# The gated delta rule of a fused kernel: from heads to tiles, from half-array to whole-array products, and part of it moved among the projections

## The chip, the cores and the metric

One core of one Trainium2 chip runs the whole program. The metric is the device time of one execution in microseconds (us), as the median of three runs. TensorE (PE) multiplies matrices, VectorE (DVE), ScalarE (ACT) and GpSimd (POOL) do the elementwise work, SyncE (SP) issues the DMAs. Each engine works through its own instructions in the order in which they were written into the program, and semaphores make it wait for others.

## What is computed

A block of two layers (gated linear attention, retention) over 2048 rows of 1024 channels, and then a second block, in which one projection feeds two branches: a gated delta rule with 4 heads of 128, in chunks of 64 rows, and an attention with 4 heads in which each row uses only the 256 keys that an index scores highest. The change is in the second block; cut to what matters:

```python
def gated_deltanet(qkv, z, b, a, conv_w, a_log, dt_bias, g_norm):
    qkv = silu(causal_conv(qkv, conv_w)); q, k, v = split(qkv, 3)
    q = l2norm(heads(q)) * DK ** -0.5; k = l2norm(heads(k)); v = heads(v)
    beta = sigmoid(b); g = -exp(a_log) * softplus(a + dt_bias)
    gc = cumsum(g, axis=-1)                 # within a chunk of 64
    decay = exp(where(causal, gc_i - gc_j, -inf))
    kb, vb = k * beta, v * beta
    lmat = where(strict, (kb @ k.T) * decay, 0)
    tmat = inverse(lmat + eye)              # triangular solve
    u, w = tmat @ vb, tmat @ (kb * exp(gc))
    attn = (q @ k.T) * decay
    qg, kg, glast = q * exp(gc), k * exp(gc_last - gc), exp(gc_last)
    def step(S, (qg, kg, u, w, attn, gl)):  # chunk after chunk
        v_new = u - w @ S
        o = qg @ S + attn @ v_new
        return S * gl + kg.T @ v_new, o
    o = rmsnorm(scan(step, 0)) * silu(z)

def dsa_sparse_attention(q_b, ckv, iq, ik, iw, ...):
    score = sum_h iw * relu(iq @ ik.T); sel = top_k(score, 256)
    p = softmax(q_b @ ckv[sel].T * R ** -0.5 + bias); o = (p @ ckv[sel]) @ w_uv * silu(z)
```

## The kernel before

The first block ends at about 1634 us of the trace. The second block (`layer2`) goes over four quarters q0 to q3 of 512 rows. In each, `begin` loads and turns the rows; `chains` makes 28 projections, each 24 matmuls of 128x512 (three per slice of 128 channels: high part by high part, low by high, high by low, so that float32r products add up to float32), and each is taken out of PSUM by ACT; then `delta` and `attention` run together; then `output` multiplies by the last weight. Weights come by DMA into buffers `wh` and `wl`, five and six of them, one projection ahead of use by the code (`ahead`), and earlier where buffers are free.

`weave` merges generators: at each turn the one that is least far along, by its steps over the number given with it, makes the next step. In `layer2` the PE's order is kept as written while projections run (`manual_schedule`); in the weave of `delta` and `attention` a scheduler places instructions. The other engines' order is the scheduler's throughout. Three weaves of projections run beside the index's scores (`index_scores`) and the search for the 256th highest score (`select`), which works on blocks 0 and 1 of a quarter, then on 2 and 3, mostly on DVE. A search ends with two `If`s for each block (L1523, L1525), which repair rare cases; DVE loads a flag and branches. What follows in DVE's order, the masks `mk` that ACT makes of the result (L1585) and with them the attention, comes behind. In the third weave (projections from number 19 or 20 to 28, 8 steps each) `start` waits until 14 steps are left, and then makes the first step of `attention` and of `delta`: loads and set-up alone, no product.

The attention goes through four blocks of 128 rows and four heads: score products L1610 into two banks `ix` (three matmuls for each piece of up to 512 keys), on DVE the sum with the mask and the maximum (L1612), on ACT the exponential; PE turns the result (L1631) and multiplies by the keys (L1641).

`delta` works head by head: for a head and all four tiles of 128 rows, `first` to `fourth` complete the inverse (L1882, L1894), turn v and k (L1890, L1907), and make u and w (L1913, L1920). When all heads are done, the recurrence runs over 4 tiles of two chunks (`cc` 0 and 1). In a chunk and for all four heads: `ws`, both w and q by the state S (L1966, 128 rows by 128 columns of the array); `vnew` on DVE, a head at a time (L1970), in the 64 partitions of this chunk; then `us`, k by vnew, on 64 rows (L1977) and `oa`, attn by vnew, on 64 rows and 64 columns (L1980), written in two loops and alternating in PE's order; then the new state on DVE (L1983). `norms` (L1263) sums squares for each head of q and k by products with one column of ones, 16 of them on 64 columns of the array each.

Of the kernel before, what the change touches and what calls it, by code (L numbers as in the profile page):

```python
# [44 lines left out]
PACE = [(6, 3, 30, 30, 14, 40)] * 4  # L45
# [16 lines left out]
class Builder:  # L62
# [784 lines left out]
    def group_b(self, ctx):  # L847
        self.pools(ctx, "b", {"pj": 2, "ix": 2, "tp": 2, "mm": 2}, 1, dict(wh=5, wl=6))
# [123 lines left out]
    def layer2(self, src, dst):  # L972
# [3 lines left out]
        self.n_g2 = 9  # L976
# [42 lines left out]
        for h in range(4):  # L1019
# [9 lines left out]
        nc.vector.memset(St, 0.0)  # L1029

        self.k = dict(cw=cw, hist=hist, nega=nega, dtb=dtb, ltri=ltri, mneg=mneg, blk=blk, chk=chk,
                      img=img, ggd=ggd, gs=gs, sh=sh, gkv=gkv, ckvN=ckvN, ckvH=ckvH, ckvL=ckvL, ikH=ikH, ikL=ikL, Tb=Tb, wuv=wuv,
                      mod=mod, src=src, dst=dst, S=St, zsel=zsel, gsel=gsel, iota=iota, under=under)
        self.mk = self.mkp.tile([P, 2048], BF16, name="mk")
        for q in range(NQ):
            pace = PACE[q]
            with self.tc.manual_schedule(engines={mybir.EngineType.PE}):
# [9 lines left out]
                self.weave((self.chains(q, st, range(x[2], 28)), 8 * (28 - x[2])), (self.select(q, st, (2, 3)), pace[3]), (self.start(att, delta, 8 * (28 - x[2]) - pace[4]), 60))  # L1047
            n = sum(4 * (1 + -(-max(0, i - 1) // 4) + 2 * -(-(i + 1) // 4)) for i in range(4 * q, 4 * q + 4))
            self.weave((delta, pace[5]), (att, n))
# [4 lines left out]
    @staticmethod  # L1054
    def image(m, h):


        return bass.AP(tensor=m.tensor, offset=m.offset + 4 * h * 129 * P, ap=[[P, P], [129 * P, 4], [1, P]])

# [20 lines left out]
    def start(self, *streams):  # L1080

        *streams, n = streams
        for _ in range(n):
            yield
        for s in streams:
            next(s)
            yield
# [89 lines left out]
    def chains(self, q, st, which):  # L1177
# [6 lines left out]
        seq += [(n, cb) for n in ("v", "za", "qb", "zb") for cb in range(4)]  # L1184
# [67 lines left out]
    def norms(self, st, h):  # L1252
# [15 lines left out]
        br, br2 = st["br"][:, :, h], st["br2"][:, :, h]  # L1268
        v.tensor_copy(st["rr"][:, :, h], r)
        v.tensor_tensor(out=br, in0=st["beta"][:, :, h], in1=r[:, 0:4], op=ALU.mult)  # L1270
        v.tensor_tensor(out=br2, in0=br, in1=r[:, 0:4], op=ALU.mult)
# [442 lines left out]
    def gates(self, st, sm):  # L1714
# [21 lines left out]
        st.update(beta=beta, g=g.rearrange("p t h -> p (t h)"), br=t16("br"), br2=t16("br2"))  # L1736

    def decays(self, st):
# [7 lines left out]
        for cc in range(2):  # L1746
            nc.tensor.matmul(gp[64 * (1 - cc):64 * (1 - cc) + 64, 64:80], c["ltri"][:, 64 * cc:64 * cc + 64], g2, start=True, stop=True)
# [4 lines left out]
        gx = self.small([P, 5, 16], "gx", bufs=1)  # L1752
        v.tensor_copy(gx, gp[:, :80].rearrange("p (j x) -> p j x", j=5))
        v.tensor_tensor(out=gx[:, 1, :], in0=gx[:, 1, :], in1=gx[:, 0, :], op=ALU.subtract)
        ge = self.small([P, 5, 16], "ge", bufs=1)
# [6 lines left out]
    def delta_products(self, st, h):  # L1762
# [17 lines left out]
        for ti in range(4):  # L1780
            sl = slice(ti * P, (ti + 1) * P)
            v.scalar_tensor_tensor(out=dc[:, sl], in0=qk[:, sl], scalar=st["rr"][:, ti, h:h + 1], in1=dc[:, sl], op0=ALU.mult, op1=ALU.mult)
# [37 lines left out]
    def delta(self, q, st):  # L1820

        nc, c = self.nc, self.k
        v = nc.vector
        sp, S = st["sp"], c["S"]
        beta, ge, n2, rr = (st[n] for n in ("br", "ge", "n2", "rr"))
        col = lambda t, ti, h: t[:, 4 * ti + h:4 * ti + h + 1]
        egc = ge[:, 0, :].rearrange("p (t h) -> p t h", h=4)
        ekg, nbeta, rin, rq = (self.small([P, 4, 4], n, bufs=1) for n in ("ekg", "nbeta", "rin", "rq"))
        for o, x, y in ((ekg, ge[:, 1, :].rearrange("p (t h) -> p t h", h=4), rr[:, 0:4, :]), (rin, n2[:, 0:4, :], rr[:, 0:4, :])):
            v.tensor_tensor(out=o, in0=x, in1=y, op=ALU.mult)  # L1830
# [94 lines left out]
        for h in range(4):  # L1925
            yield
            if h < 3:
                load(h + 1)
# [144 lines left out]
```

## Time and profile before

| what | value |
|---|---|
| median of three runs | 3402.31 us (3400.49 to 3407.59) |
| profiled execution | 3399.2 us, its span 3397.2 us |
| mean granted TensorE clock | 0.968 |
| PE busy | 3232.6 us, 95% of the span |
| DVE, ACT, POOL busy | 1921.7, 1178.5, 1065.1 us |
| q0: projections / attention and delta rule | 1633.9 to 1833.7 / to 1953.5 us |
| q1 | 2002.0 to 2231.7 / to 2370.2 us |
| q2 | 2424.0 to 2671.2 / to 2814.5 us |
| q3 | 2876.0 to 3137.4 / to 3319.6 us, the end at 3397.2 |

The table is read from the times, the page's first part, and from where the last matmul of the projections (L1190) and the first of the output (L210) start. A matmul of float32 is two records in the trace, one of float32r is one; a busy time of PE has overlap in it, so that prices are best read from the distance between starts.

### The profile page before, as it was taken

To read this page: it belongs to the slowest core of one execution; us is meant where nothing else is said; L and a number is where in the kernel's file an instruction comes from. 1 tells how busy PE (TensorE), PEld (TensorE's weight loads), DVE (VectorE), ACT (ScalarE), POOL (GpSimd) and SP (SyncE) were. 2 spreads that over 40 slices of the span, in tenths; PEclk is the share of its full clock that TensorE was granted. 3 is DMA by queue.
4 is the path that set the end of the run, shared out by engine and by line. 5 is a ranking of instruction groups with operands and counts; after the bars stand their busy time and mean duration, and the time that the engine had idled before them with its cause. 6 is when DMAs were issued, how large, how long until landed. Compare 5 with 4: busy or idle time off the path is not lost. (4 is left out here: it accounts for less than half of the span.)

```text
span 3397.2 us, 46405 instructions
## 1 busy us (share of the span) xinstructions
PE 3232.6 (95%) x16946; PEld 2625.8 (77%) x16946; DVE 1921.7 (57%) x5192; ACT 1178.5 (35%) x1977; POOL 1065.1 (31%) x917
## 2 busy tenths in 40 slices
PE   8999999999989999999998999979998999998898
PEld 5878877788877787878787778767786778776877
DVE  2236455244514742245576557865588865698953
ACT  4222243122322322212332324334254443553542
POOL 3123361232553546452221122512116112134111
PEclk9999999999999999999998899989999999999899
DMA  4112247123536725212668255652545705436302
GB/s 123 34 44 97 96 138 269 48 81 115 186 98 217 265 88 192 93 48 101 219 232 246 65 198 193 198 166 80 174 165 166 210 14 187 167 131 209 99 32 75
DMA packets 352727, 472.39 MB, mean 139 GB/s; under 512 B 80867, under 2 KB 235699, under 8 KB 351446
## 3 DMA queue, kind: packets, MB, share of 16 engines
q1 hardware_dynamic: 352470, 469.20, 42.2%
q8 instruction: 133, 2.18, 0.3%
q14 instruction: 124, 1.02, 0.1%
HBM read 365.13 MB, written 103.99 MB: 138 GB/s over the span
## 5 line engine op out<-in xcount | busy, mean ns | idle before, releaser
L144 POOL TENSOR_TENSOR wl<-wr,wh 128x1024 fp32r<-128x1024 f32 x126 | 299.8, 2383 | 561.7 <-ACT wh L143 550.2
L210 PE MATMUL pj<-wh,xh 128*128 128x512 f32 x1024 | 403.0, 396 | 10.5 <-ACT wh L143 9.6
L210 PE MATMUL pj<-wl,xh 128*128 128x512 f32 x1024 | 404.2, 395 | 3.8 <-POOL wl L144 3.8
L199 PE MATMUL pj<-xh,wh 128*128 128x512 f32 x992 | 397.9, 401 | 8.3 <-ACT wh L143 5.9
L210 PE MATMUL pj<-wh,xl 128*128 128x512 f32 x1024 | 403.1, 394 | 0.0
L199 PE MATMUL pj<-xh,wl 128*128 128x512 f32 x992 | 393.7, 397 | 0.0
L199 PE MATMUL pj<-xl,wh 128*128 128x512 f32 x992 | 393.6, 397 | 0.0
L1190 PE MATMUL pj<-xh,wh 128*128 128x512 f32 x896 | 360.3, 402 | 17.7 <-ACT spl L1217 9.4
L1190 PE MATMUL pj<-xl,wh 128*128 128x512 f32 x896 | 355.9, 397 | 9.9 <-DVE xl L165 3.8
L1190 PE MATMUL pj<-xh,wl 128*128 128x512 f32 x896 | 354.8, 396 | 0.0
L143 ACT CAST wh<-wr 128x1024 fp32r<-128x1024 f32 x126 | 130.5, 1038 | 438.9 <-PE pj L210 143.5
L210 PEld LDWEIGHTS pj<-wh,xh 128*128 128x128 f32 x1024 | 193.8, 189 | 53.3 <-ACT wh L143 10.4
L199 PEld LDWEIGHTS pj<-xh,wh 128*128 128x128 f32 x992 | 183.8, 185 | 61.5 <-ACT wh L143 7.7
L210 PEld LDWEIGHTS pj<-wl,xh 128*128 128x128 f32 x1024 | 193.9, 189 | 45.5 <-POOL wl L144 5.8
L210 PEld LDWEIGHTS pj<-wh,xl 128*128 128x128 f32 x1024 | 193.9, 189 | 40.6 <-issue 0.8
L199 PEld LDWEIGHTS pj<-xl,wh 128*128 128x128 f32 x992 | 183.7, 185 | 46.2 <-issue 4.5
L199 PEld LDWEIGHTS pj<-xh,wl 128*128 128x128 f32 x992 | 183.3, 185 | 45.8 <-issue 3.2
L1190 PEld LDWEIGHTS pj<-xh,wh 128*128 128x128 f32 x896 | 170.7, 191 | 56.0 <-ACT spl L1217 10.2
L1190 PEld LDWEIGHTS pj<-xl,wh 128*128 128x128 f32 x896 | 170.9, 191 | 47.3 <-DVE xl L165 5.6
L1353 ACT ACTIVATE relu<-ix 128x512 f32<-128x512 f32 (+3 forms) x266 | 143.3, 543 | 184.8 <-PE ix L1347 122.2
L1354 DVE SCALAR_TENSOR_TENSOR score<-relu,iwc,score 128x512 f32<-128x512 f32 (+3 forms) x266 | 191.7, 721 | 19.5 <-ACT relu L1353 16.3
L1190 PEld LDWEIGHTS pj<-xh,wl 128*128 128x128 f32 x896 | 170.7, 190 | 37.8
(542 smaller groups left out, 6479.7 us busy)
## 6 DMA issues: line engine op xcount, KB each, us to landing
wh<-kh SPq DMA_DIRECT2D x140, 512.0 KB, 4.4
wl<-kl SPq DMA_DIRECT2D x140, 512.0 KB, 5.0
wr<-in_l_w_in_dram SPq DMA_DIRECT2D x92, 512.0 KB, 3.7
kh<-wh SPq DMA_DIRECT2D x37, 512.0 KB, 3.6
kl<-wl SPq DMA_DIRECT2D x37, 512.0 KB, 4.5
wr<-in_l_w_out_dram SPq DMA_DIRECT2D x32, 512.0 KB, 3.6
x<-y SPq DMA_DIRECT2D x32, 512.0 KB, 2.6
wr<-in_w_in_dram SPq DMA_DIRECT2D x29, 512.0 KB, 4.8
```

The costliest lines, as they stand in the source:

```text
L143: nc.scalar.copy(wh, raw)
L144: nc.gpsimd.tensor_tensor(out=wl, in0=raw, in1=f(wh), op=ALU.subtract)
L199: self.nc.tensor.matmul(ps[:m, :], a[:, k, :], b[tb][k], start=(n == 0), stop=(n == 3 * KT - 1))
L210: self.nc.tensor.matmul(ps, a[tb][k][:, o:o + P], b[:, k % 2, :], start=(n == 0), stop=(n == 3 * KT - 1))
L1190: nc.tensor.matmul(ps, a[:, k, :], b[0][k], start=k + n == 0, stop=k == KT - 1 and n == 2)
L1353: nc.scalar.activation(t[:, :m], ps[:, :m], AF.Relu)
L1354: nc.vector.scalar_tensor_tensor(out=o, in0=t[:, :m], scalar=w, in1=o, op0=ALU.mult, op1=ALU.add)
```

## The change

The delta rule goes tile by tile: for a tile of 128 rows and all four heads `first` to `fourth` prepare, and the recurrence of a tile follows its own preparation, with the next tile's four preparing steps placed between its chunk's steps. `us` takes all 128 rows: k is kept in two copies, `kg0` and `kg1`, each with zeros in the rows of the other chunk, and `vnew` lies in two fixed buffers of 128 partitions. `oa` is made once for a tile, on 128 rows and 128 columns, after its second chunk. `vnew` is one subtraction for all heads on DVE, since beta now stands in the factors of k, `attn` and u; u leaves PSUM by an ACT copy. `norms` takes 8 products on 128 columns instead of 16 on 64; `decays` loses two products. The loads go by tile too. `wh` and `wl` lose one buffer each, and small buffers go from 9 to 11. In the third weave `part` waits 4 steps and then makes 10 steps of `attention`, and waits 20 and then makes 6 of `delta`; these use the banks `ix` where `delta` used `pj`. The projection of `qb` moves ahead of `za`.

```diff
-PACE = [(6, 3, 30, 30, 14, 40)] * 4
+PACE = [(6, 3, 30, 30, 10, 40, 20, 6)] * 4
...
-        self.pools(ctx, "b", {"pj": 2, "ix": 2, "tp": 2, "mm": 2}, 1, dict(wh=5, wl=6))
+        self.pools(ctx, "b", {"pj": 2, "ix": 2, "tp": 2, "mm": 2}, 1, dict(wh=4, wl=5))
...
-                self.weave((self.chains(q, st, range(x[2], 28)), 8 * (28 - x[2])), (self.select(q, st, (2, 3)), pace[3]), (self.start(att, delta, 8 * (28 - x[2]) - pace[4]), 60))
...
+                self.dtag = "ix"
+                m = 8 * (28 - x[2])
+                self.weave((self.chains(q, st, range(x[2], 28)), m), (self.select(q, st, (2, 3)), pace[3]),
+                           (self.part(att, 4, pace[4]), 4 + pace[4]), (self.part(delta, pace[6], pace[7]), pace[6] + pace[7]))
+            self.dtag = "pj"
+            self.weave((delta, 40 - pace[7]), (att, sum(n) - pace[4]))
...
-        seq += [(n, cb) for n in ("v", "za", "qb", "zb") for cb in range(4)]
+        seq += [(n, cb) for n in ("v", "qb", "za", "zb") for cb in range(4)]
...
-                for cc in range(2):
-                    o = 64 * (cc ^ n)
-                    nc.tensor.matmul(ss[o:o + 64, 4 * n + ti:4 * n + ti + 1], sq[:, ti * P + 64 * cc:ti * P + 64 * cc + 64],
-                                     self.ones[:, 0:1], start=True, stop=True)
+                nc.tensor.matmul(ss[:, 4 * n + ti:4 * n + ti + 1], sq[:, ti * P:(ti + 1) * P], self.ones[:, 0:1], start=True, stop=True)
...
+            for o, x in ((T["k"], egc), (T["kg0"], ekg[:, 0]), (T["kg1"], ekg[:, 1])):
+                v.tensor_tensor(out=h4(o), in0=h4(tp), in1=by_head(x, ti), op=ALU.mult)
...
+        for fn in (first, second, third, fourth):
+            fn(0)
+            yield
...
-                vn = self.g2("vnew")
-                for h in range(4):
-                    sl = slice(h * P, (h + 1) * P)
-                    v.scalar_tensor_tensor(out=vn[a, sl], in0=ws[a, sl], scalar=nb2[a, 4 * ti + h:4 * ti + h + 1],
-                                           in1=UB[h][a, ti * P:(ti + 1) * P], op0=ALU.mult, op1=ALU.add)
-                nc.scalar.copy(on[b, :], ws[b, :])
+                v.tensor_tensor(out=vn[a, :], in0=T["ub"][a, :], in1=ws[a, :], op=ALU.subtract)
+                nc.scalar.copy(on[a, :], ws[b, :])
                 yield
-                us = self.psum("pj")
-                for h in range(4):
-                    sl = slice(h * P, (h + 1) * P)
-                    nc.tensor.matmul(us[:, sl], KG[h][a, ti * P:(ti + 1) * P], vn[a, sl], start=True, stop=True)
-                for h in range(4):
-                    sl = slice(h * P, (h + 1) * P)
-                    nc.tensor.matmul(oa[b, sl], AT[h][a, ti * P + 64 * cc:ti * P + 64 * cc + 64], vn[a, sl], start=True, stop=True)
+                for fn in itertools.islice(ahead_of, 1):
+                    fn(ti + 1)
+                    yield
+                us = self.psum(self.dtag)
+                for sl in heads:
+                    nc.tensor.matmul(us[:, sl], T["kg0" if cc == 0 else "kg1"][:, sl], vn[:, sl], start=True, stop=True)
...
+                if cc == 1:
+                    oa = self.psum("mm")
+                    for sl in heads:
+                        nc.tensor.matmul(oa[:, sl], T["at"][:, sl], vn[:, sl], start=True, stop=True)
```

How the instructions of three places move. In the rows a name before the arrow is what is written, those behind it are read; a number at a name's end tells buffers apart, xN is N of the same, and ISA is an instruction that the listing has no name for. First PE in q0's recurrence, one chunk of four heads before (`us` L1977, `oa` L1980):

```order
L1977 MATMUL pj_14610<-vnew_14589,kg_14223 128x128
L1980 MATMUL mm_14583<-vnew_14589,at_14220 64x128
L1977 MATMUL pj_14610<-vnew_14589,kg_14223 128x128
L1980 MATMUL mm_14583<-vnew_14589,at_14220 64x128
L1977 MATMUL pj_14610<-vnew_14589,kg_14223 128x128
L1980 MATMUL mm_14583<-vnew_14589,at_14220 64x128
L1977 MATMUL pj_14610<-vnew_14589,kg_14223 128x128
L1980 MATMUL mm_14583<-vnew_14589,at_14220 64x128
L1631 MATMUL tp_15002<-ident,P_14730 128x128 x3
L1966 MATMUL pj_14629<-dS_14619,wq_14210 128x128 x2
```

and after the change (`ws` L1950, `us` L1959, `oa` L1968; L1879 to L1906 prepare the next tile, L1619 is the attention):

```order
L1950 MATMUL pj_14481<-dS_14418,dt_14295 128x128 x4
L1879 MATMUL pj_14515<-T_14471,ms_14469 128x64 x4
L1959 MATMUL pj_14526<-vnew_11744,dt_14295 128x128 x4
L1886 MATMUL pj_14542<-ident,v_14475 128x128 x4
L1890 MATMUL pj_14548<-Y_14473,T_14471 128x64 x4
L1950 MATMUL pj_14570<-dS_14531,dt_14295 128x128 x4
L1619 MATMUL ix_14560<-ckvH,qh_14501 128x128
L1619 MATMUL ix_14565<-ckvH,qh_14501 128x256
L1900 MATMUL pj_14582<-ident,k_14477 128x128 x4
L1619 MATMUL ix_14560<-ckvH,ql_14502 128x128
L1619 MATMUL ix_14560<-ckvL,qh_14501 128x128
L1619 MATMUL ix_14565<-ckvH,ql_14502 128x256
L1619 MATMUL ix_14565<-ckvL,qh_14501 128x256
L1968 MATMUL mm_14613<-vnew_11744,at_14448 128x128 x4
L1906 MATMUL pj_14591<-v_14475,Y_14473 128x128 x4
L1959 MATMUL pj_14603<-vnew_11744,kg_2041_14397 128x128 x4
```

The alternation of two products is gone; `us` stands four in a row, `oa` four in a row behind every second one, with preparation and attention in between.

Second, PE in q3 where the projections end: before, all of the attention's score products (L1610) stand behind the last projection (L1190):

```order
L1190 MATMUL pj_30152<-xh_26645,wh_30094 128x512
L1190 MATMUL pj_30152<-xl_26647,wh_30094 128x512
L1523 UNCONDITIONAL_BRANCH
L1190 MATMUL pj_30152<-xh_26645,wl_30095 128x512
L1523 UNCONDITIONAL_BRANCH
L1610 MATMUL ix_30923<-ckvH,qh_30178 128x512
L1610 MATMUL ix_30928<-ckvH,qh_30178 128x512
L1610 MATMUL ix_30923<-ckvH,ql_30179 128x512
L1610 MATMUL ix_30923<-ckvL,qh_30178 128x512
L1610 MATMUL ix_30928<-ckvH,ql_30179 128x512
```

After, the third score product of the first head (L1619, bank `ix_29785`) stands within the fourth projection from the end (L1202); some 93 matmuls of projections follow it:

```order
L1202 MATMUL pj_29781<-xl_26446,wh_29708 128x512
L1202 MATMUL pj_29781<-xh_26444,wl_29709 128x512
L1532 UNCONDITIONAL_BRANCH x2
L1619 MATMUL ix_29785<-ckvH,qh_29615 128x384
L1619 MATMUL ix_29785<-ckvH,ql_29616 128x384
L1619 MATMUL ix_29785<-ckvL,qh_29615 128x384
L1202 MATMUL pj_29781<-xh_26444,wh_29708 128x512
L1202 MATMUL pj_29781<-xl_26446,wh_29708 128x512
```

The first two score products are earlier still. The bank of the third is that of the first, `ix_29671`, and DVE must have read that. Third, DVE's order after the change at that place: the first reading of `ix_29671` (L1621) stands behind both `If`s of blocks 0 and 1 (L1532, L1534):

```order
L1534 UNCONDITIONAL_BRANCH x2
L1532 UNCONDITIONAL_BRANCH
L1529 ISA x2
L1387 TENSOR_TENSOR t_s_29399<-t_s_29399,t_sl_29400 128x2
L1621 ISA P_29669,at_mx_29670<-ix_29671,mk 128x512
L1621 ISA at_mx_29670 128x1
L1621 ISA P_29669,at_mx_29670<-ix_29746,mk 128x512
L1621 ISA at_mx_29670 128x1
```

So a product that stood behind the projections now stands among them, and still behind the same `If`s.

## Rows read from the trace of the kernel before

**Rows 1.** Four windows: bounds, length, busy us (count) by engine, PEclk, DMA share, GB/s.

```profile
1833.70:1953.50 119.80, 100.11 (x589) 81.49 (x588) 58.62 (x217) 38.86 (x116) 23.69 (x29) 0.79 0.36 111
2231.70:2370.20 138.50, 121.40 (x782) 104.22 (x781) 85.67 (x315) 55.48 (x135) 24.39 (x26) 0.88 0.31 92
2671.20:2814.50 143.30, 134.84 (x963) 117.30 (x962) 105.66 (x371) 72.16 (x151) 25.03 (x27) 0.96 0.32 98
3137.40:3319.60 182.20, 161.48 (x1139) 143.25 (x1137) 132.21 (x434) 93.92 (x175) 29.07 (x31) 0.91 0.26 78
```

**Rows 2.** Timeline of PE, q0: start, busy us, line, tiles, rows*columns, shape, count.

```profile
1925.44 1.06 PE L1966 MATMUL pj<-dS,wq 128*128 128x128 f32 x8
1926.34 0.83 PE L1641 MATMUL mm<-PT,ckvN 128*128 128x128 f32 x6
1927.10 0.48 PE L1977 MATMUL pj<-vnew,kg 64*128 64x128 f32 x2
...
1930.20 0.66 PE L1945 MATMUL pj<-ident,on 128*128 128x128 f32 x4
```

**Rows 3.** Timeline of PE, q0, an earlier chunk.

```profile
1895.41 0.79 PE L1977 MATMUL pj<-vnew,kg 64*128 64x128 f32 x2 [0.45 <-DVE vnew L1970]
...
1900.75 1.65 PE L1966 MATMUL pj<-dS,wq 128*128 128x128 f32 x6
```

**Rows 4.** Timeline of PE, q3, eight records of L1977 in a run.

```profile
3265.28 1.16 PE L1977 MATMUL pj<-vnew,kg 64*128 64x128 f32 x8
3266.37 0.43 PE L1980 MATMUL mm<-vnew,at 64*64 64x128 f32 x2
```

**Rows 5.** Timeline of PE, q0, products of decays and of norms between projections.

```profile
1672.82 0.29 PE L1745 MATMUL tp<-gg__1641_11966,ltri 128*128 128x16 f32 x2
...
1673.71 0.29 PE L1747 MATMUL tp<-gg__1641_11966,ltri 128*64 128x16 f32 x4
...
1701.37 0.39 PE L1190 MATMUL pj<-xl,wh 128*128 128x512 f32 x1
1701.59 0.39 PE L1190 MATMUL pj<-xh,wl 128*128 128x512 f32 x1
1701.91 1.10 PE L1263 MATMUL tp<-ones,ext 128*64 128x1 f32 x32
1702.94 0.50 PE L1190 MATMUL pj<-xh,wh 128*128 128x512 f32 x1
```

**Rows 6.** DVE by line, 1833.7 to 3319.6 us: busy, mean ns, idle ahead.

```profile
L1970 DVE SCALAR_TENSOR_TENSOR vnew<-pj,nbeta,ub 64x128 f32<-64x128 f32 x128 | 37.2, 348 | 22.9 <-PE pj L1966 22.6
L1983 DVE SCALAR_TENSOR_TENSOR dS<-dS,ge,pj 128x128 f32<-128x128 f32 x128 | 35.9, 344 | 60.6 <-PE pj L1977 60.6
...
L1211 DVE TENSOR_TENSOR iq<-pj,iq 64x512 fp32r<-64x512 f32 x24 | 16.5, 690 | 25.5 <-ACT iq L1210 25.3
```

**Rows 7.** ACT by line, from 1633.9 us on.

```profile
L1234 ACT ACT_TABLE_LOAD x8 | 10.3, 1283 | 0.1
```

**Rows 8.** PE's waits in q0's window: total, times, longest us.

```profile
PE ix L1610 <- DVE at_mx L1612: 11.6, 1, 11.6
```

**Rows 9.** Timeline of DVE, q0, where PE waits in rows 8.

```profile
1846.81 0.29 DVE L1612 CUSTOM_DVE_ANT_0 P<-ix,near 128x128 f32<-128x128 f32 x1 [13.04 <-DMA T<-img]
```

**Rows 10.** Timelines of PE and DVE, q2, behind the first pair's search.

```profile
2658.86 0.50 PE L1190 MATMUL pj<-xh,wh 128*128 128x512 f32 x1 [3.81 <-ACT spl L1217]
...
2661.03 0.17 DVE L1383 TENSOR_SCALAR t_m<-t_dc 128x2 int32<-128x2 f32 x1 [2.82 <-DVEq L1523]
```

**Rows 11.** Timelines of PE and DVE, q3, behind the first pair's search.

```profile
3137.40 0.39 PE L1190 MATMUL pj<-xh,wl 128*128 128x512 f32 x1
3151.83 1.22 PE L1610 MATMUL ix<-ckvH,qh 128*128 128x512 f32 x2 [14.04 <-ACT qh L164]
...
3154.46 0.69 DVE L1612 CUSTOM_DVE_ANT_0 P<-ix,mk 128x512 f32<-128x512 f32 x1
```

**Rows 12.** The page, part 6: issues, KB each, median us to landing.

```profile
wh<-kh SPq DMA_DIRECT2D x140, 512.0 KB, 4.4
```

More of the change, by code (lines that the diff above doesn't have):

```diff
@@ L1078, in woven, with part @@
                 yield
-    def start(self, *streams):
-        *streams, n = streams
+    @staticmethod
+    def part(stream, wait, n):
+        for _ in range(wait):
+            yield
         for _ in range(n):
-            yield
-        for s in streams:
-            next(s)
+            next(stream)
             yield
@@ L1886, in second, with h4 @@
-        def second(h):
-            Th, Yh, vt = heads[h]
-            tp = self.psum("pj")
-            for sl in tiles:
-                nc.tensor.transpose(tp[:, sl], vt[:, sl], self.ident)
-            v.tensor_tensor(out=t4(vt), in0=t4(tp), in1=rin[:, :, h:h + 1].to_broadcast([P, 4, P]), op=ALU.mult)
-            cp = self.psum("pj")
-            for ti, sl in enumerate(tiles):
-                nc.tensor.matmul(half(cp, ti), Th[:, sl], some(Yh, 1)[:, ti], start=True, stop=True)
+        def h4(ap):
+            return ap.rearrange("p (h i) -> p h i", h=4)
@@ new lines, in first, with second @@
+        def first(ti):
+            T = tiles[ti]
+            ap = self.psum(self.dtag)
+            for h, sl in enumerate(heads):
+                nc.tensor.matmul(half(ap, h), T["ms"][:, sl], some(T["T"], 0)[:, h], start=True, stop=True)
+            nc.scalar.copy(some(T["T"], 0), halves(ap))
+        def second(ti):
+            T = tiles[ti]
+            tp = self.psum(self.dtag)
+            for sl in heads:
+                nc.tensor.transpose(tp[:, sl], T["v"][:, sl], self.ident)
+            v.tensor_tensor(out=h4(T["v"]), in0=h4(tp), in1=by_head(rin, ti), op=ALU.mult)
+            cp = self.psum(self.dtag)
+            for h, sl in enumerate(heads):
+                nc.tensor.matmul(half(cp, h), T["T"][:, sl], some(T["Y"], 1)[:, h], start=True, stop=True)
@@ L1916, in fourth @@
-        def fourth(h):
-            Yh, vn, kn = heads.pop(h)
-            wp = self.psum("pj")
-            for sl in tiles:
-                nc.tensor.matmul(wp[:, sl], kn[:, sl], Yh[:, sl], start=True, stop=True)
-            for cc in range(2):
-                nc.scalar.copy(WQ[h][:, cc::2, 64 * cc:64 * cc + 64], wp.rearrange("p (n s) -> p n s", s=64)[:, cc::2, :])
-        first(0)
-        for h in range(4):
-            yield
-            if h < 3:
-                load(h + 1)
-            second(h)
-            yield
-            if h < 3:
-                first(h + 1)
-            third(h)
-            yield
-            fourth(h)
-            yield
@@ new lines, in fourth @@
+        def fourth(ti):
+            T = tiles[ti]
+            wp = self.psum(self.dtag)
+            for sl in heads:
+                nc.tensor.matmul(wp[:, sl], T["k"][:, sl], T["Y"][:, sl], start=True, stop=True)
+            for cc in range(2):
+                nc.scalar.copy(T["wq"][:, :, cc, 64 * cc:64 * cc + 64], h4(wp)[:, :, 64 * cc:64 * cc + 64])
+            T["at"] = self.g2("at")
+            nc.sync.dma_start(h4(T["at"]), sp["at"][:, :, ti * P:(ti + 1) * P])
+        def out(ti, on):
+            tp = self.psum(self.dtag)
+            for sl in heads:
+                nc.tensor.transpose(tp[:, sl], on[:, sl], self.ident)
+            ts = slice(ti * P, (ti + 1) * P)
+            z = self.g2("za")
+            nc.sync.dma_start(h4(z), sp["za"][:, :, ts])
+            v.tensor_tensor(out=z, in0=tp, in1=z, op=ALU.mult)
```

183 lines of the change are left out of this document (80 added, 103 removed).

## Prediction

> **What bounds the kernel now.** PE is busy almost throughout; DVE and ACT are not, so a gain has to come from PE's work, from its waits, or from the clock that it is granted. I read first the windows by stage [rows 1]: one row for each quarter, from the last projection to the first product of the output, where PE, DVE and the granted clock stand side by side. In these four windows of 583.8 us in all PE is busy 517.8 and DVE 382.3; the granted clock is 0.79, 0.88, 0.96 and 0.91. [...]
>
> Then PE's timeline in one chunk of the recurrence [rows 2]. The reader is to see that the eight products of `us` and `oa`, alternating between 64 rows by 128 columns and 64 by 64, take from 1927.10 to 1930.20, 3.10 us, while four products on the whole array (`ws`, eight records) take from 1925.44 to 1926.34, 0.90 us. The same `us` in an undisturbed run of eight records takes 1.09 us [rows 4], so its 64 rows aren't slow in themselves; the turn from one shape to the other is. At the low level the same chunk takes from 1895.41 to 1900.75, 5.34 us [rows 3].
>
> Last, the waits behind the search. In q0 PE waits 11.6 us for DVE [rows 8], which itself stands 13.04 us ahead of its first work for the attention [rows 9]. The trace names a DMA of T there, which that reduction does not read; two branches of the search stand in DVE's order at that place. In q2 PE waits 3.81 us among the projections, and DVE goes on at 2661.03 after a branch [rows 10]. In q3 PE ends the projections at 3137.40, waits 14.04 us, and DVE's first attention work starts at 3154.46 [rows 11].
>
> **The change part by part.** *Products.* 32 chunks of 3.10 us are 99.2 us. After: 32 times four `us` and 16 times four `oa` on the whole array, 48 times 0.90 = 43.2 us. That is −56 us [rows 2], at full clock. Ends: −65 (the price of a shape change may also go at the neighbours), −40 (if every second group still pays 0.5 us for standing alone, 32 times).
>
> *Norms.* 32 records on 64 columns take 1.03 us; after, 16 records on 128 columns. The nearest rows are L1745's eight records on 128 columns in 0.89 us, 111 ns each: 16 of them are 1.78 us, so +0.75 us, times 16 bursts +12 us [rows 5]. The other end is 0, if a record is priced by its columns (128 instead of 64, half as many). I take +12, since no 128-column row here is cheaper than 111 ns.
>
> [...]
>
> *The clock.* In q0 PE runs chunks at the low level though it has products all the time [rows 3]. A chunk there costs 2.24 us more than at full clock. I credit 8 of the 32 chunks: −18 us. Ends: 0 (another stretch is at the low level instead) and −64 (all of it goes, rows 1).
>
> *Float32 among float32r.* A projection's matmul that precedes a float32 product takes 0.32 us to the next start instead of 0.22 [rows 5]; I estimate as much for the way back, 0.2 us for each insertion. 16 steps in each of four quarters, of which perhaps two thirds stand apart, make 43 insertions: +8 us. Ends: 0 and +13.
>
> *Waits behind the search.* PE works in order, and the third score product now stands 93 matmuls ahead of the projections' end. It needs the bank of the first, whose reader on DVE comes behind the `If`s. In q3 PE gets there at about 3137.4 − 93 × 0.22 [rows 5] = 3116.9, plus some 8 us (an estimate) of work inserted by then, 3125. DVE gets there about 3149, 5 us ahead of 3154.46, since PE's first products after its wait are then done beforehand [rows 11]. So 24 us of waiting take the place of 14.0: +10. In q2 the projections end at 2671.2 [rows 1]; less 93 × 0.22 and the wait of 3.8, plus 8, PE is there at 2655, and DVE some 2 us of small steps behind 2661.03, at 2663: 8 us in place of 3.8, +4 [rows 10]. In q0 there is no search of blocks 0 and 1, but the delta rule's prepared factors wait for DVE behind the search of blocks 2 and 3: the 11.6 us stay, 0 [rows 8, 9]. q1 I leave at 0. Sum +14; ends −20 (the work now ahead of the wait lets DVE catch up in q0 and q1) and +49 (below). Behind the waiting product stand the projections, their evacuations on ACT and, through the banks, the weights' DMAs; all have slack as long as PE stands still.
>
> *A closer dependence.* `us` now waits for one subtraction of 64x512 on DVE (0.69 us, as L1211) where it followed head by head, and `ws` for four L1983 (4 × 0.344 = 1.4) as before [rows 6]. `us` after it is 0.90. Two handovers of about 0.1 added, a chunk is at least 0.9 + 0.7 + 0.9 + 1.4 + 0.2 = 4.1 us, eight of them 33 us in a quarter, far below the windows. PE has to find 0.7 us of other work for `vnew` and 1.4 for the state. In q1 to q3 the attention gives it; in q0 it has least of that. 8 chunks of up to 2.1 us are 17; I take half, +8. Ends 0 and +29 (14 chunks).
>
> *At nothing.* Twenty more table loads on ACT of 1.283 us [rows 7] (26 us over four quarters) and sixteen more copies: ACT is busy 260 of 584 us in these windows [rows 1]. If the cover goes, one on the path of an evacuation costs 1.3. DVE loses 128 subtractions of 0.348 and gains 32 of 0.69 [rows 6], −22 us of an engine that isn't the bound. Four instead of five buffers `wh`: projections of 24 × 0.22 = 5.3 us [rows 5] mean that four buffers, three of them ahead, leave some 16 us, against 4.4 us to the landing of one [rows 12]. Without that cover each late weight would cost its excess over 16 us. The loads by tile go through SP, whose queue only issues; the next tile's are asked for a whole tile, two chunks or 8 us, ahead.
>
> **Sum.** −56 + 12 − 18 + 8 + 14 + 8 = −32 us. From 3399.2 that is 3367.2; the profiled execution is 3.1 us below the median of the runs, so 3370 us.
>
> **Rivals.** *Low: waits and clock go as well.* What speaks for it is that PE's waits and its low level occur together [rows 3, 8]. Then norms 0, q0's 25 us and half of the other 39, together −45, waits and dependence 0, switches +8: −56 − 45 + 8 = −93, 3309 us. Against it is the order, which leaves DVE's stops in place. Chance 0.16.
>
> *The recurrence sets the pace.* If PE finds nothing for the 2.1 us of a chunk in all of q0 and in every fourth chunk after it, 14 in all, the dependence costs 29 instead of 8: −11, 3391 us; from 19 chunks on nothing is gained. For it: PE already waits in q0 with less demand. Against it: PE's share in q2 and q3 [rows 1]. Chance 0.12.
>
> *Slower: PE in order behind the search.* The score product stands still in q1 and q2 for 14 us more than now, as PE does in q3 before, and in q3 for 24 more: 52. The 93 matmuls behind each wait then begin at the low level; if half of their 20 us runs there, 10 each are lost, 30. 82 in place of +14 makes −32 + 68 = +36, 3438 us. It decides from the point where waits and clock behind them cost over 46 us; up to there, from 39 on, the result is no change. For it: a wait of 14.04 us in q3 that only grows [rows 11]. Against it: the projections wait no worse than the attention does now. Chance 0.16, half of it no change.
>
> *Rows don't matter.* If a product costs by its columns alone, a tile's eight `us` and sixteen half-width products become eight and four whole ones with the same sum of columns: products 0, norms 0, and no clock to credit. +8 + 14 + 8 = +30, 3432 us. [Rows 2, 4] speak against it: the alternating products take 3.10 us where such a sum gives 1.3. Chance 0.03. [...]
>
> **How the numbers follow.** The forecast, 3370 us, has 0.53, with a range of its own from 3345 to 3390. Below it lies 0.16, above it 0.31. The range over the cases is 3318 to 3408: it takes in part of the low rival, the recurrence's and the no-change case, and leaves about one in ten at either end. What a measurement can tell from no change is 0.2%, 7 us. Faster: 0.53 + 0.16 + 0.12, less 0.02 for the forecast's edge, 0.79; no change 0.08 and that edge's 0.01, 0.09; slower 0.08 + 0.03 and 0.01, 0.12.
>
> **What would show it.** Right: four `us` take 0.9 us wherever they stand; the windows of attention and delta rule shrink by about 20 us in q0 and less in q3, while the windows of the projections grow by 8 to 25; a PE wait of 20 us or more among q3's last projections; norms' bursts of 1.8 us; the granted clock of q0's window above 0.85. Wrong: bursts of 1.0 us, a wait in q3 that stays at 14 or vanishes, or `us` waiting over 1 us for DVE in most chunks. The prediction fails most if DVE's stops come at another time than before, since +14 rests on times of the old trace.

## The result and the profile after

The changed kernel takes 3367.45 us (median of 4 runs, 3363.85 to 3370.53) where the kernel before took 3401.91: a ratio of 0.9896, 95% interval 0.9883 to 0.9908. The forecast was 3370, faster. The profiled execution took 3370.5 us with a span of 3368.8; its clock is 0.971 on average, 0.968 before. So the sum came out. Its terms did so only in part, and some were missing.

The windows of attention and delta rule of the changed kernel, from the last projection to the output, q0 to q3 as in [rows 1]:

```profile
1872.40:1940.70 68.30, 61.87 (x513) 58.04 (x511) 51.41 (x176) 39.92 (x106) 20.45 (x22) 1.00 0.59 181
2231.90:2326.50 94.60, 84.98 (x686) 80.85 (x685) 70.38 (x238) 53.46 (x127) 24.51 (x25) 0.98 0.43 130
2658.50:2773.90 115.40, 108.75 (x863) 104.41 (x862) 80.64 (x264) 66.45 (x143) 23.58 (x25) 0.97 0.34 104
3149.40:3296.50 147.10, 136.50 (x1055) 128.53 (x1054) 99.29 (x300) 82.06 (x159) 26.64 (x28) 0.97 0.29 86
```

They are 51.5, 43.9, 27.9 and 35.1 us shorter than before; the clock in them is 1.00, 0.98, 0.97 and 0.97. But work has moved out of them. The windows of the projections, first of the kernel before, then of the changed one (the first row of each begins where the first block ends: before, at the first transpose of the second block's rows, after the change at the end of the first block's last product):

```profile
1633.90:1833.70 199.80, 194.12 (x1002) 158.68 (x1003) 134.71 (x491) 71.59 (x127) 33.57 (x27) 0.98 0.77 249
2002.20:2231.70 229.50, 213.51 (x1079) 173.40 (x1078) 171.30 (x572) 97.36 (x183) 75.82 (x107) 0.97 0.59 197
2424.20:2671.20 247.00, 229.04 (x1142) 183.39 (x1142) 198.20 (x585) 115.83 (x205) 83.31 (x106) 0.97 0.54 179
2875.90:3137.40 261.50, 246.98 (x1207) 195.42 (x1205) 222.54 (x575) 133.39 (x226) 80.40 (x104) 0.98 0.51 170
```

```profile
1633.45:1872.40 238.95, 209.51 (x996) 174.03 (x997) 155.04 (x542) 85.28 (x150) 41.17 (x40) 0.93 0.70 225
1987.70:2231.90 244.20, 226.53 (x1078) 185.25 (x1077) 183.82 (x623) 109.14 (x199) 79.41 (x110) 0.97 0.58 191
2380.20:2658.50 278.30, 246.96 (x1141) 198.62 (x1140) 218.85 (x662) 129.51 (x223) 85.44 (x109) 0.94 0.51 167
2835.30:3149.40 314.10, 270.10 (x1216) 214.06 (x1215) 256.73 (x686) 151.43 (x250) 86.46 (x108) 0.92 0.44 148
```

These are 39.2, 14.7, 31.3 and 52.6 us longer, and their clock falls from 0.97 or 0.98 to between 0.92 and 0.97. Together, a quarter is 29 us shorter in q1, 3 longer in q2 and 17 longer in q3; q0 is 12 us shorter, or 29 if counted from its first projection. The span is 28 us shorter; what the quarters leave of that lies in the outputs behind them, 5 us in q3's. In q0 the difference is that PE now stands still between the two blocks:

```profile
1633.06 0.39 PE L210 MATMUL pj<-wh,xl 128*128 128x512 f32 x1
1647.64 0.45 PE L1127 MATMUL tp<-ident,xr 128*128 128x128 f32 x1 [14.19 <-issue]
```

The last product of the first block (L210) starts at 1633.06, the first transpose of the second block's rows (L1127) at 1647.64 after 14.19 us; before it started at 1633.90. SP issues the loads of these rows here:

```profile
1633.53 2.06 SPq L1106 DMA_DIRECT2D xr<-x  x4
```

In the kernel before, it issued them 79 us earlier, and the first transpose waited 0.78 us:

```profile
1554.29 1.82 SPq L1094 DMA_DIRECT2D xr<-x  x4
1633.90 0.66 PE L1115 MATMUL tp<-ident,xr 128*128 128x128 f32 x4 [0.78 <-DVE score L1503]
```

The explanation, tested below: the change had made the weights' pool two buffers smaller, and the row buffers behind it slid over buffers that the first block still used, presumably those of its last weights.

The new products behave as forecast. In q2, `us` of four heads (eight records) starts at 2693.54 and the next at 2694.43, 0.89 us [rows 2: 0.90 for `ws`]:

```profile
2693.54 1.06 PE L1959 MATMUL pj<-vnew,dt 128*128 128x128 f32 x8
2694.43 0.60 PE L1886 MATMUL pj<-ident,v 128*128 128x128 f32 x4
```

A burst of norms on 128 columns takes from 1715.10 to 1716.80, 1.70 us, for 1.03 [rows 5]:

```profile
1715.10 1.84 PE L1273 MATMUL tp<-ones,ext 128*128 128x1 f32 x16
1716.80 0.49 PE L1202 MATMUL pj<-xh,wh 128*128 128x512 f32 x1
```

And in q3 PE waits among the projections for the first score product's reader, 21.52 us against 14.04 in [rows 11]:

```profile
3114.45 0.69 PE L1619 MATMUL ix<-ckvH,qh 128*128 128x384 f32 x1 [21.52 <-DVE at_mx L1621]
3114.94 0.52 PE L1619 MATMUL ix<-ckvH,ql 128*128 128x384 f32 x1
```

In q2 the same wait is 10.17 us. Ahead of it the first score product waits 8.97 us for `qh`, the high part of the queries, which ACT makes:

```profile
2601.71 0.80 PE L1619 MATMUL ix<-ckvH,qh 128*128 128x512 f32 x1 [8.97 <-ACT qh L164]
2624.62 0.58 PE L1619 MATMUL ix<-ckvH,qh 128*128 128x256 f32 x1 [10.17 <-DVE at_mx L1621]
```

In q0 the delta rule's prepared factors take the place of the attention's wait of 11.6 us [rows 8]. The row of L1879 names a load; the row of L1900 names DVE's scaling of v, which stands behind the search of blocks 2 and 3 (total, times, longest us):

```profile
PE ix L1900 <- DVE v L1887: 4.7, 1, 4.7
PE ix L1879 <- DMA T<-img: 4.4, 1, 4.4
```

### The profile page after: what moved, and what is told of

The parts are those of the page before. It is cut to its first block, busy times and chain, and to the rows that moved or that the text cites. A ratio compares the mean times of both kernels' runs of the same rounds, so it can differ in the third digit from the quotient of the medians.

```text
span 3368.8 us, 45610 instructions
## 1 busy us (share of the span) xinstructions
PE 3171.5 (94%) x16546; PEld 2608.0 (77%) x16546; DVE 1912.2 (57%) x5082; ACT 1215.1 (36%) x2013; POOL 1071.8 (32%) x917
## 5 line engine op out<-in xcount | busy, mean ns | idle before, releaser
L210 PE MATMUL pj<-wh,xh 128*128 128x512 f32 x1024 | 402.9, 396 | 9.7 <-ACT wh L143 8.6
L210 PE MATMUL pj<-wl,xh 128*128 128x512 f32 x1024 | 404.1, 395 | 4.2 <-POOL wl L144 4.2
L210 PE MATMUL pj<-wh,xl 128*128 128x512 f32 x1024 | 403.2, 394 | 0.0
L1202 PE MATMUL pj<-xl,wh 128*128 128x512 f32 x896 | 361.0, 403 | 10.3 <-DVE xl L165 5.6
L1202 PE MATMUL pj<-xh,wh 128*128 128x512 f32 x896 | 366.6, 409 | 0.2 <-PE pj L1202 0.2
L1202 PE MATMUL pj<-xh,wl 128*128 128x512 f32 x896 | 359.5, 401 | 0.0
L210 PEld LDWEIGHTS pj<-wh,xh 128*128 128x128 f32 x1024 | 193.8, 189 | 52.8 <-ACT wh L143 9.4
L210 PEld LDWEIGHTS pj<-wl,xh 128*128 128x128 f32 x1024 | 193.9, 189 | 45.8 <-POOL wl L144 6.1
L210 PEld LDWEIGHTS pj<-wh,xl 128*128 128x128 f32 x1024 | 193.8, 189 | 40.5 <-issue 0.8
L1202 PEld LDWEIGHTS pj<-xl,wh 128*128 128x128 f32 x896 | 174.3, 194 | 48.2 <-DVE xl L165 8.3
L1202 PEld LDWEIGHTS pj<-xh,wl 128*128 128x128 f32 x896 | 173.4, 194 | 39.1
L1202 PEld LDWEIGHTS pj<-xh,wh 128*128 128x128 f32 x896 | 174.3, 194 | 36.6 <-PE pj L1202 1.3
```

The source lines that it names most:

```text
L210: self.nc.tensor.matmul(ps, a[tb][k][:, o:o + P], b[:, k % 2, :], start=(n == 0), stop=(n == 3 * KT - 1))
L1202: nc.tensor.matmul(ps, a[:, k, :], b[0][k], start=k + n == 0, stop=k == KT - 1 and n == 2)
```

## The experiments

Each starts from the changed kernel. Ratios, with their intervals, are to the kernel before on the same chip; times are medians. The kernel before took 3401.7 to 3403.1 us beside them, so the medians can be set against each other, but executions of one kernel lie up to 18 us apart, and differences of a few us say little.

**Rows loaded early.** A table of 8 KB is placed ahead of the row buffers, which moves these back to where they were.

```diff
-        ckvN = C([P, NT, P], "ckvN")
+        ckvN = self.mkp.tile([P, NT, P], F32, name="ckvN")
```

> The changed kernel, with one table of the second block (ckvN, 8 KB of a partition) placed ahead of the buffers for the rows instead of behind them, so that these buffers lie where they lay in the kernel before. Theory: the 14.2 us for which PE stands still between the two blocks come from the rows being loaded only at 1633.5 us, because two weight buffers less let the rows' buffers slide over two buffers of the first block's last weights; then the rows load near 1560 us again, the gap goes, and the time is 14 to 16 us lower, about 3352 us. Rival: the gap comes from the order of the DMA queue or of DVE, whose program changed; then the gap stays and the time is that of the changed kernel, 3367.

3362.42 us, 0.9877 (0.9843 to 0.9911). Loads and first transpose:

```profile
L1106 SPq DMA_DIRECT2D xr<-x x4: 338/427/514, 1556.5 to 1557.9; - x4
```

```profile
1636.12 0.66 PE L1127 MATMUL tp<-ident,xr 128*128 128x128 f32 x4 [0.78 <-DVE score L1512]
```

The loads are issued from 1556.5 us, and the gap of 14.19 is 0.78: the theory of the place holds, the rival falls. The time is only 5 us lower, inside the intervals: q0 gives part of the gap back, where the wait of 4.7 us for DVE is now 9.8:

```profile
PE ix L1900 <- DVE v L1887: 9.8, 1, 9.8
```

DVE ends its last step of the search 11.6 us sooner (at 1841.7 instead of 1853.3 us), but then stands 15.41 us instead of 10.87 before it scales v. First the changed kernel, then this one:

```profile
1864.22 0.69 DVE L1887 TENSOR_TENSOR v<-ix,rin 128x512 f32<-128x512 f32 x1 [10.87 <-DMA T<-img]
```

```profile
1857.15 0.69 DVE L1887 TENSOR_TENSOR v<-ix,rin 128x512 f32<-128x512 f32 x1 [15.41 <-DMA v<-sp_v]
```

In both, DVE's queue is at the branches of the search's `If`s (L1532) in that time. Why the stop is longer here is not shown.

**Norms on 64 columns.**

```diff
-                nc.tensor.matmul(ss[:, 4 * n + ti:4 * n + ti + 1], sq[:, ti * P:(ti + 1) * P], self.ones[:, 0:1], start=True, stop=True)
+                for cc in range(2):
+                    o = 64 * cc
+                    nc.tensor.matmul(ss[o:o + 64, 4 * n + ti:4 * n + ti + 1], sq[:, ti * P + o:ti * P + o + 64],
+                                     self.ones[:, 0:1], start=True, stop=True)
```

> The changed kernel, with the norms' products on 64 columns as before (16 instead of 8 for each head). Theory: a burst falls from 1.84 to 1.03 us, 16 bursts, 13 us lower, about 3354 us, since projections stand on both sides of them and nothing hides them. Rival: an array's columns are loaded at a price by their number and the 1.84 us were lengthened by waits for the squares; then a burst doesn't change and the time is 3367.

3350.62 us, 0.9860 (0.9827 to 0.9893): 17 us below the changed kernel, 13 expected. The 16 bursts account for 11 (0.67 us each); the intervals don't tell the two apart. The burst is 1.03 us again, with 32 records:

```profile
1711.34 1.10 PE L1275 MATMUL tp<-ones,ext 128*64 128x1 f32 x32
1712.37 0.50 PE L1202 MATMUL pj<-xh,wh 128*128 128x512 f32 x1
```

**Nothing early.** Only loads and set-up are made ahead, 14 steps before the projections end.

```diff
-                           (self.part(att, 4, pace[4]), 4 + pace[4]), (self.part(delta, pace[6], pace[7]), pace[6] + pace[7]))
+                           (self.part(att, m - 14, 1), 60), (self.part(delta, m - 14, 1), 60))
...
-            self.weave((delta, 40 - pace[7]), (att, sum(n) - pace[4]))
+            self.weave((delta, 40 - 1), (att, sum(n) - 1))
```

> The changed kernel, but with the attention and the delta rule kept out of the projections as before: only their loads and set-up are issued 14 steps ahead of the end. Theory: the products' gain stays whole; q0 and q1, which gained 29 us each, lose some 15 and 10 of it again, q2 and q3 lose the waits of 10 and 21 us among the projections and the low clock behind them, -12 and -25 us; in sum about -12, 3355 us. Rival: the early start carries the gain, the products only a little; then 3385 us or more.

3345.12 us, 0.9828 (0.9796 to 0.9861): 22 us below the changed kernel. The early start costs, by more than was expected. The windows of attention and delta rule:

```profile
1849.90:1947.60 97.70, 77.95 (x575) 72.67 (x574) 57.15 (x201) 41.50 (x121) 25.21 (x30) 0.88 0.52 160
2225.80:2335.40 109.60, 96.19 (x755) 92.25 (x753) 79.66 (x287) 56.60 (x139) 26.70 (x28) 0.95 0.46 139
2634.40:2772.60 138.20, 122.10 (x924) 115.42 (x923) 108.84 (x383) 77.75 (x160) 26.47 (x28) 0.91 0.36 106
3103.90:3273.30 169.40, 149.72 (x1133) 140.33 (x1131) 131.75 (x410) 96.00 (x180) 31.98 (x32) 0.93 0.31 91
```

They are longer than the changed kernel's by 29, 15, 23 and 22 us, but the projections ahead of them are shorter by 22, 13, 33 and 45:

```profile
1633.45:1849.90 216.45, 197.85 (x933) 163.79 (x934) 148.16 (x518) 72.35 (x127) 36.71 (x32) 0.94 0.73 233
1994.60:2225.80 231.20, 217.89 (x1011) 177.50 (x1010) 170.63 (x574) 97.18 (x181) 77.52 (x107) 0.96 0.58 189
2388.90:2634.40 245.50, 233.67 (x1075) 187.92 (x1073) 190.53 (x542) 112.73 (x200) 81.41 (x106) 0.97 0.53 178
2834.80:3103.90 269.10, 250.38 (x1139) 197.96 (x1137) 224.01 (x575) 133.99 (x228) 82.95 (x104) 0.97 0.48 162
```

In these two profiles the early start thus gains 7 us in q0 and 2 in q1, and loses 10 in q2 and 23 in q3. The first two are near chance: the run with two score products (below) leaves q0 as in the changed kernel, and there q0 takes 359.1 us from the first block's last product to q1's first projection, in the changed kernel 354.6. The wait in q3 is back behind the projections, and smaller than 21.5:

```profile
PE ix L1619 <- ACT qh L164: 9.9, 1, 9.9
PE ix L1619 <- DVE at_mx L1621: 6.9, 1, 6.9
```

**Alternating products.** `us` on 64 rows and `oa` on 64 by 64 for each head in turn, kept in that order.

```diff
+            oa = self.psum("mm")
...
-                for sl in heads:
-                    nc.tensor.matmul(us[:, sl], T["kg0" if cc == 0 else "kg1"][:, sl], vn[:, sl], start=True, stop=True)
+                with self.tc.manual_schedule(engines={mybir.EngineType.PE}):
+                    for sl in heads:
+                        nc.tensor.matmul(us[:, sl], T["kg0" if cc == 0 else "kg1"][a, sl], vn[a, sl], start=True, stop=True)
+                        nc.tensor.matmul(oa[a, sl], T["at"][a, sl.start + 64 * cc:sl.start + 64 * cc + 64], vn[a, sl], start=True, stop=True)
...
-                if cc == 1:
-                    oa = self.psum("mm")
-                    for sl in heads:
-                        nc.tensor.matmul(oa[:, sl], T["at"][:, sl], vn[:, sl], start=True, stop=True)
```

> The changed kernel, with the products of a chunk put back as they were: for each head one us on 64 rows and one oa on 64 rows and 64 columns, alternating, in an order that PE keeps. Theory (a change of shape costs): a chunk takes 3.1 us at full clock again instead of 0.9 and half of 0.9, 1.75 us more, 32 chunks, +56 us, about 3423 us, more where the clock falls; less what PE's waits for DVE cover. Rival (price by columns): the same sum of columns, 3367 us. Another rival (the recurrence or DVE sets the pace of these windows): between, about 3385 us.

3440.57 us, 1.0116 (1.0082 to 1.0150): 73 us above the changed kernel. The chunk takes from 2699.93 to 2703.02, 3.09 us:

```profile
2699.93 0.48 PE L1961 MATMUL pj<-vnew,dt 64*128 64x128 f32 x2
2700.34 0.43 PE L1962 MATMUL mm<-vnew,at 64*64 64x128 f32 x2
...
2703.02 1.16 PE L1650 MATMUL mm<-PT,ckvN 128*128 128x128 f32 x8
```

The 56 us of the products are not all of it. The mean clock is 0.967 over a span of 3441.4 us where the changed kernel has 0.971 over 3368.8: one minus the clock, times the span, is 114 and 98 us, 16 more. 56 + 16 = 72. This reckoning is an estimate, since it also counts time at the low level, a granted clock of 0.50, in which PE stands still; half of the time that PE is busy at that level (158 and 130 us in the two traces) differs by 14.

**`us` on 64 rows, undisturbed.** Four heads in a row, `oa` as after the change.

```diff
-                    nc.tensor.matmul(us[:, sl], T["kg0" if cc == 0 else "kg1"][:, sl], vn[:, sl], start=True, stop=True)
+                    nc.tensor.matmul(us[:, sl], T["kg0" if cc == 0 else "kg1"][a, sl], vn[a, sl], start=True, stop=True)
```

> The changed kernel, with us taken on the chunk's own 64 rows, four heads in a row, and all else as it is (oa once a tile on the whole array). Theory (not the rows cost, but each turn from one shape to another): four products in a row take 1.1 instead of 0.9 us, 64 groups, so at most +13 us, 3367 to 3380 us. If 64 rows in themselves were slow, as the alternating chunk suggests, it would be 2 x 3.1 / 2 - 0.9 for each group or more, +40 us, above 3400. Price by columns alone: 3367.

3380.35 us, 0.9935 (0.9916 to 0.9954): 13 us above the changed kernel.

```profile
2665.77 1.16 PE L1959 MATMUL pj<-vnew,dt 64*128 64x128 f32 x8
2666.86 0.65 PE L1886 MATMUL pj<-ident,v 128*128 128x128 f32 x4
```

Eight records take 1.09 us, 0.2 more than on 128 rows. From the second record on they start 0.11 us apart, as they do on 128 rows; the 0.2 lie at the ends, 0.21 us from the first start to the second and 0.20 from the last to the next product. Ahead of the first there is 0.1 more, 0.21 us instead of 0.11. So it isn't the 64 rows that cost, nor the columns, but the turn from one shape to another. The expectation counted 64 groups; there is one in each of 32 chunks, and 32 times 0.3 are 9 us, with which the 13 agree within the intervals.

**Two score products.** In q2 and q3 the attention's early steps end ahead of the third.

```diff
-PACE = [(6, 3, 30, 30, 10, 40, 20, 6)] * 4
+PACE = [(6, 3, 30, 30, 10, 40, 20, 6)] * 2 + [(6, 3, 30, 30, 3, 40, 20, 6)] * 2
```

> The changed kernel, in which the attention's early steps in q2 and q3 stop after the set-up and the first two score products, so that the third, which needs a bank back from DVE, stands behind the projections; the delta rule's early steps stay. Theory (this product is what PE waits at): the waits of 10 and 21 us leave the projections, PE's low clock there with them, and about half comes back behind the projections; 10 to 18 us lower, 3350 to 3357 us. Rival (the delta rule's second and third step wait behind the same search just as long): 3367.

3342.38 us, 0.9819 (0.9800 to 0.9837): 25 us below the changed kernel, more than expected, and level with nothing early. The edit does more than drop the third product. With fewer steps to spread over the projections, `weave` also makes the others later: in q3 the first score product starts 24 us before the projections end instead of 69, the second behind them. So the 25 us are not those of the third product alone; q2's wait for `qh` is gone too. The rival is right in part, for products of the delta rule now wait among the projections, 11.0 us in q2, as long as the third score product did, and 9.0 in q3:

```profile
PE ix L1879 <- DMA T<-img: 11.0, 1, 11.0
```

```profile
PE ix L1890 <- DVE at_mx L1621: 9.0, 1, 9.0
```

**All three.** Rows early, norms on 64 columns, nothing early: the three diffs above together.

```diff
+        ckvN = self.mkp.tile([P, NT, P], F32, name="ckvN")
...
+                           (self.part(att, m - 14, 1), 60), (self.part(delta, m - 14, 1), 60))
...
+            self.weave((delta, 40 - 1), (att, sum(n) - 1))
...
+                    nc.tensor.matmul(ss[o:o + 64, 4 * n + ti:4 * n + ti + 1], sq[:, ti * P + o:ti * P + o + 64],
...
```

> The changed kernel with the three earlier changes at once: rows loaded early, norms on 64 columns, nothing but loads ahead among the projections. If they add up (6 or 7 us from the rows, since q0's search gives back the rest; 15 from the norms; 22 from the order): 3324 us. If the order was what made the search give back the rows' gain in q0, the rows bring 14 instead of 6: 3316. If norms and rows shift only the moment at which PE waits for the search: 3340.

3313.17 us, 0.9737 (0.9716 to 0.9758), the fastest: 54 us below the changed kernel. The numbers fit a sum of 17, 22 and 14 or 15, so without the early start the rows seem to bring their whole 14; that they do so was not run by itself.

**Early in q0 and q1 only**, otherwise as all three.

```diff
...
-                           (self.part(att, 4, pace[4]), 4 + pace[4]), (self.part(delta, pace[6], pace[7]), pace[6] + pace[7]))
+                           *([(self.part(att, m - 14, 1), 60), (self.part(delta, m - 14, 1), 60)] if q >= 2 else
+                             [(self.part(att, 4, pace[4]), 4 + pace[4]), (self.part(delta, pace[6], pace[7]), pace[6] + pace[7])]))
...
-            self.weave((delta, 40 - pace[7]), (att, sum(n) - pace[4]))
+            self.weave((delta, 40 - (1 if q >= 2 else pace[7])), (att, sum(n) - (1 if q >= 2 else pace[4])))
...
```

> As the one with all three, but with the early start of attention and delta rule kept in q0 and q1 and dropped in q2 and q3. Compared by quarter, the changed kernel is 7.5 us shorter with it in q0 and 2 in q1, and 10 and 23 us longer in q2 and q3. Theory (early start pays where DVE's search is short): 8 to 10 us below the one with all three. Rival (the end of the search sets q0 whatever PE does ahead): the same as that one.

3320.89 us, 0.9755 (0.9737 to 0.9774): 8 us slower than all three, where 8 to 10 faster was expected. The theory falls. In the profiles q0 takes 344.2 us from the first block's last product, 340.1 in all three, and q1 takes 390.4 against 384.6, so the early start loses here what it seemed to gain. That its gain in q0 depended on the late rows fits this, but is not shown apart from chance and from the norms.

**Two score products, rows early, norms on 64 columns.**

```diff
+PACE = [(6, 3, 30, 30, 10, 40, 20, 6)] * 2 + [(6, 3, 30, 30, 3, 40, 20, 6)] * 2
...
+        ckvN = self.mkp.tile([P, NT, P], F32, name="ckvN")
...
+                    nc.tensor.matmul(ss[o:o + 64, 4 * n + ti:4 * n + ti + 1], sq[:, ti * P + o:ti * P + o + 64],
...
```

> Rows loaded early, norms on 64 columns, and the early start kept but with only two score products ahead in q2 and q3. If the three add up (25, 17 and 6 to 14 us): 3312 to 3320 us, level with the one that puts nothing ahead. If PE reaches the search's end sooner and waits there, 3325 or more.

3320.26 us, 0.9765 (0.9746 to 0.9783): at the upper edge of what was expected, and 7 us behind all three, with intervals that overlap.

**Tiles alone.** All three, and the alternating products.

```diff
+        ckvN = self.mkp.tile([P, NT, P], F32, name="ckvN")
...
+                           (self.part(att, m - 14, 1), 60), (self.part(delta, m - 14, 1), 60))
...
+                    nc.tensor.matmul(ss[o:o + 64, 4 * n + ti:4 * n + ti + 1], sq[:, ti * P + o:ti * P + o + 64],
...
+                        nc.tensor.matmul(us[:, sl], T["kg0" if cc == 0 else "kg1"][a, sl], vn[a, sl], start=True, stop=True)
+                        nc.tensor.matmul(oa[a, sl], T["at"][a, sl.start + 64 * cc:sl.start + 64 * cc + 64], vn[a, sl], start=True, stop=True)
...
```

> What is left of the change when the whole-array products, the norms, the early start and the rows' late load are all undone: the delta rule by tiles instead of heads, vnew by one instruction, the other order of the projections, the table loads. Theory (all that the prediction costed stands in these four): the time of the kernel before, 3402 us, within 8. Rival (going by tiles shortens the windows too, since the recurrence begins after one tile's preparation): by the runs so far 3313 plus 73, 3386 us.

3393.86 us, 0.9972 (0.9962 to 0.9982): 9 us below the kernel before, just outside the theory's 8 and halfway to the rival. From one quarter's first projection to the next one's, the two profiles differ by −2, −14, +10 and +3 us, so the 9 us are a balance. The windows of q0 and q3, first of this kernel, then of all three, which differs from it by the products alone:

```profile
1829.70:1950.20 120.50, 101.21 (x606) 86.55 (x605) 61.20 (x203) 42.31 (x121) 27.25 (x32) 0.79 0.45 135
3134.60:3326.40 191.80, 168.25 (x1194) 146.85 (x1193) 136.12 (x416) 98.17 (x182) 30.20 (x32) 0.93 0.27 81
```

```profile
1828.00:1922.00 94.00, 73.59 (x574) 69.72 (x573) 56.49 (x201) 41.98 (x121) 24.41 (x29) 0.89 0.54 167
3064.40:3237.90 173.50, 149.62 (x1132) 140.66 (x1132) 131.11 (x412) 96.73 (x181) 32.19 (x32) 0.91 0.29 88
```

With alternating products q0's window is 120.5 us at a clock of 0.79, as before the change [rows 1]; with whole-array products it is 94.0 at 0.89. The whole difference between the two kernels is 81 us, measured on two chips.

## Why the prediction was right

**Products and clock: −56 − 18 = −74 forecast, −73 and −81 measured.** Both rows on which this rested were right: 0.89 for 0.90 us, and 3.09 for 3.10 when the old order is put back. The low level on which the forecast counted is a granted clock of 0.50 in the chunk of [rows 3], against 1.00 in that of [rows 2]. The clock went as forecast: 16 us in one pair of kernels. By the same reckoning it is 105 (0.031 of 3393.7) against 83 (0.025 of 3310.2) in the other, 22 us; by half of PE's busy time at the low level the two pairs give 14 and 27. Between the two kernels of the change 109 − 98 = 11 us came back. In the four windows it went from 64 us (25, 17, 6 and 16, as the clocks and lengths of [rows 1] give them) to 10, but in the projections it rose from some 23 to 66, behind the new waits and in part during them, where PE stands still and loses nothing by it: in q3 the clock is 0.50 from 3096.8 to 3117.3 us, and PE's wait ends at 3114.5. By PE's busy time at the low level (164 and 130 us) 17 came back.

**Norms: +12 forecast, bursts +0.67 (11 us for 16), 17 when undone.** The row L1745 was the right one.

The forecast's other end, a price by the sum of columns, would have given 0; the sum is the same, and a burst went from 1.03 to 1.70 us. Records on 128 columns start 0.112 us apart; on 64 columns, before the change, they start in pairs, 0.007 us within a pair and 0.058 from one pair to the next, and the code writes these products into the two halves of the 128 output partitions in turn. What makes the pairs is not shown. Rows made no difference within a run: records on 64 and on 128 rows start 0.11 us apart.

**Waits and float32 among float32r: +14 + 8 = +22 forecast, the early start costs 22.** The place was right: the third score product waits 21.5 us in q3 (24 forecast) and 10.2 in q2 (8). That the sum is hit to the microsecond is luck: the 9.0 us for which the first score product waits in q2, 5.0 us in q1, which had been left at 0, and what work done early saves behind the projections stood in no term, and the low clock in and behind the waits (the projections' window of q3 went from 0.98 to 0.92) had been left to a rival. More work moved than the prediction's signs allowed for: they had the attention's windows about 20 us shorter and the projections 8 to 25 longer, and these became 28 to 52 shorter and 15 to 53 longer. Holding the attention's early products back to the end of the projections in q2 and q3 gives 25 us. The 8 us for the change of type were not measured by themselves.

**A closer dependence: +8 forecast, not seen.** PE's waits at `us` for `vnew` are 1.5 us in all. The two handovers of a chunk, put at about 0.1 us each, had 0.1 together in [rows 3]: PE stood 0.45 us there, and one subtraction takes 0.348 [rows 6]. What is left when the four known parts are undone is 9 us faster than before; which of its edits brings that stays open.

**At nothing: this step failed.** Two weight buffers less were costed by how far ahead a load can be issued, and that cover held. What they did was to move addresses: the rows' buffers came to lie on buffers still in use, the loads came 77 us later (1633.5 instead of 1556.5 with the place restored), and PE stood 14.2 us. In the changed kernel about 5 of these are net: with the rows early, DVE's longer stop in q0 takes 4.5 back, and the rest isn't told from chance.

So the number was hit in part because errors cancel: about 5 us net for the rows and 5 more for the norms, which the sum lacked, against 8 of a dependence that did not come and 9 that the rest of the change gains. Put right, −32 becomes −39; −34.5 was measured, 3401.9 to 3367.5.

**The rivals.** The low case did not come with this change, though its level, 3309 us, is nearly that of the kernel with all three parts put right. The recurrence as pace and the price by the sum of columns fall with the alternating products. The slower rival described what happened in q2 and q3, at a price that stayed below the gain. One sum of the prediction is off by a digit: DVE is busy 382.2 us in the four windows, not 382.3.

## What to carry to other kernels

Look at what small matrix products stand next to: here the turns from one shape of the array to another made a chunk's products take 3.1 us instead of 1.3 (0.9 and half of 0.9), and filling the array with zeros was worth 73 to 81 us, clock included. Work that is moved among other work on an engine that keeps its order carries its waits along, here 21.5 us among q3's projections, so ask of every moved instruction what must be ready, and when. And when a pool changes its size, ask what now lies on which address: here a load came 77 us later without any line of its own having changed.

## What was not expected of the hardware

Products with a single moving column on 128 columns of the array took 106 ns a record (1.70 us for 16) and on 64 columns, with the outputs in the two halves of the partitions in turn, 32 ns (1.03 for 32); these start in pairs, 58 ns from pair to pair. Eight records on 64 rows took 0.2 us more than eight on 128 when others stand before and behind them, all of it at the two ends of the run. And in q0 more than half the gain of the denser products lies in the clock, by an estimate from its window's length and clock: the same window became 26.5 us shorter and went from 0.79 to 0.89 when nothing but the shape of its products changed, which by one minus the clock, times the length, is 25 against 10 us.
